# Rows of streamed operands at one byte of a 128-byte line

## Chip, cores, metric

One core of one Trainium2 chip. The metric is the device time of one execution in microseconds; the median of several runs counts.

## What is computed

Two blocks of a transformer over x of 256 rows and 1024 channels, all in float32. The first block has two layers, each a SwiGLU feed-forward, a mixer (a pooling mixer in the first layer, native sparse attention in the second), cross attention to a memory of 256 rows, and a second feed-forward. The second block has one layer: three kinds of attention side by side, gated and merged, and a feed-forward with squared ReLU. Cut to what carries the time:

```python
def swiglu_ffn(h, w_in, w_out):
    g, u = jnp.split(h @ w_in, 2, axis=-1)
    return (jax.nn.silu(g) * u) @ w_out

for i in range(2):
    x = x + 0.5 * swiglu_ffn(rms_norm(x, ffn1_norm[i]), ffn1_w_in[i], ffn1_w_out[i])
    x = x + mixer(rms_norm(x, mix_norm[i]))
    x = x + memory_cross_attention(rms_norm(x, xattn_norm[i]), rms_norm(mem, mem_norm[i]), ...)
    x = x + 0.5 * swiglu_ffn(rms_norm(x, ffn2_norm[i]), ffn2_w_in[i], ffn2_w_out[i])
# second block: u @ w_in feeds three attentions and their gates, then
h = jnp.square(jax.nn.relu(u2 @ w_ff1))
x = x + gate2 * (h @ w_ff2)
```

## The kernel before

Activations stand transposed: channels on the 128 partitions, the 256 rows of x on the free axis. Weights come from HBM in slabs of 1 MB (`raw`, L114), eight tiles of 128 channels by 256 columns, over SyncE's queue. ScalarE rounds a half slab to float32r (`wh`, L98), VectorE subtracts that from the slab (`wl`, L104). A float32 product is then three matmuls, `mm3` (L154, its matmuls are L157 to L159): `wh` with the activations' high part, `wh` with their low part, `wl` with the high part. In each the weight tile of 128 x 128 is loaded first, and the activations, 128 partitions x 256 columns, are streamed; the load for the next matmul runs beside the matmul that streams. A few products have it the other way round, with the activations loaded and the weights streamed (`row_tiles`, L603).

The activations that most slabs take are `xsh` and `xsl`, eight tiles (k = 0 to 7) of 256 columns. They lie in the pool `ac`, in a tile with two more columns in each row (`wide`, L283), which only the second block uses: there a product takes 258 columns. So row k begins 258 x 4 = 1032 bytes behind row k - 1. `pair` (L277) hands out such a tile for the tag `xs` and a packed one, 1024 bytes from row to row, for all others: `xs2h`/`xs2l` of the second block, `msh`/`msl` of the memory, `qT`. Temporaries of a phase come from `tmp` (L61): `hh`/`hl`, the inner activations of a feed-forward, `h2h`/`h2l` of the last one, `pTh`/`pTl`, `vh`/`vl` and `oh`/`ol` of the cross attention, and in the last feed-forward `xsh`/`xsl` too, packed.

Pools lie one behind the other in SBUF: `cst` (constants; its last tile is `fgg`, L1126), `wp` (slabs and split weights), `ac`, the pools of a block, and the pool of a phase. Inside a pool each tile takes its size, rounded up to 32 bytes a partition; a tag with two buffers has them side by side. Adding these up gives the byte at which rows begin. It is shown in a 128-byte line, and as the distance from the loaded weight tile to the streamed row, modulo 512 bytes (weight tiles are 512 bytes wide, so one number holds for all of a slab):

| operand, streamed | byte in the line | distance to the weights |
|---|---|---|
| `wh`, `wl` (loaded) | 96 | |
| `xsh` row k, `xsl` row k, wide | 96 + 8k, 32 + 8k | 8k, 64 + 8k |
| `hh`, `hl`, and packed `xsh`, `xsl` of the last feed-forward | 32 | 320 |
| `oh`, `ol` of the cross attention | 32 | 64 |
| `ms` of the merge | 32 | 192 |
| `xs2`, `ms` of the memory, `nsa_oh` | 96 | 128 |
| `h2h`, `h2l`, `nsa_ol` | 96 | 384 |
| `pTh`, `pTl` with `vh`, `vl` loaded, each with the next load | 32 (weights 32) | 0 |

In a feed-forward (`_swiglu`, L381) slab j goes: 96 matmuls with `xs` (for each of the eight k two column tiles of the gate and the up half, three matmuls each), then 48 with `hh`/`hl` of slab j - 2 (`output`, L410). The order of the work on each engine is the order of the program text; nothing in it depends on where tiles lie, except that a tile which takes another's place waits for that one's last reader.

Of the kernel before, what the change touches and what calls it, by code (L numbers as in the profile page):

```python
# [15 lines left out]
P = 128  # L16
# [4 lines left out]
F2 = 4096  # L21
EPS = 1e-6
# [4 lines left out]
class Slab:  # L27
    """A split weight slab in parts of n of its rows of tiles: (hi, lo) of columns c of row k."""
# [11 lines left out]
class Net:  # L40
    """Activations live transposed (channels on partitions, rows on the free axis). A float32
    product is three float32r passes over exactly split operands: hi*hi + lo*hi + hi*lo."""
# [18 lines left out]
    def tmp(self, shape, dtype=F32, tag="t", bufs=None, pool=None):  # L61
        kw = {} if bufs is None else {"bufs": bufs}
        return (pool or self.tp).tile(shape, dtype, tag=tag, name=self.name(tag), **kw)
# [5 lines left out]
    def phase(self, name, banks=0):  # L69
        """Temporaries of one phase, and PSUM banks beside the four of self.pm."""  # L70
# [9 lines left out]
    @contextmanager  # L80
    def banks(self, n):
        """n PSUM banks beside the four of self.pm, for one phase."""
        with self.tc.tile_pool(name=self.name("pa"), bufs=n, space=bass.MemoryType.PSUM) as pool:
            yield pool

    def fill(self, n=1):
        """Trace n steps of the work that waits for a gap on the tensor engine."""
# [26 lines left out]
    def raw(self, src, shape):  # L114
        """A weight slab as it is."""
# [10 lines left out]
    def slab(self, src, shape, perm=(None, None)):  # L126
        """A weight slab [128, ...], at most 8 KB a partition, from DRAM and split."""
        return self.split_slabs([self.raw(src, shape)], perm)[0]

    def split_slabs(self, raws, perm=(None, None), turn=1):  # L130
        """Slabs of one shape that are used side by side; turn = -1: from the last rows on."""
# [5 lines left out]
    def halves(self, raw, src=None, dst=None):  # L137
        """(hi, lo) of a part of a slab; src and dst give the views that are split one by one."""
# [15 lines left out]
    def mm3(self, out, w, x, start, stop, skip=True):  # L154
        """out += w.T @ x for split w and x."""
# [6 lines left out]
    def setup(self):  # L162
        """Constants, and x: transposed, and split for the first layer's feed-forward."""
# [10 lines left out]
        # the activation tables come while x does  # L174
# [4 lines left out]
        with self.phase("setup", 4) as px:  # L179
            # tiles k and k + 2 share a bank  # L180
# [11 lines left out]
            for h in range(2):  # L192
                # x's tiles and the slabs' parts in the order of their use
# [12 lines left out]
    def first_slabs(self):  # L206
        """The first slabs of the first feed-forward, in halves as they are needed."""
# [7 lines left out]
    def setup2(self):  # L215
# [12 lines left out]
        # rows that see no compressed block, and the blocks a row doesn't see  # L228
# [11 lines left out]
    def load_rows(self, src, dst):  # L240
        """[1, 256, 1024] of DRAM into dst [128, 8, 256], transposed."""
# [17 lines left out]
    def vector_columns(self, nm, vr):  # L259
        """Vectors of DRAM as columns: entry [p, i] of a vector's block is its value i*128+p."""  # L260
# [8 lines left out]
    def transpose2(self, dst, srcs):  # L269
        """dst [128, len(srcs)*128] from [128, 128] blocks."""  # L270
# [12 lines left out]
    def wide(self, tag, dtype):  # L283
        """Eight tiles of 256 columns and two more."""
        return self.ac.tile([P, KT, S + 2], dtype, tag=tag, name=self.name(tag))

# [1 line left out]
    def split(self, src, gain=None, tag="xs", pool=None, order=None):  # L288
        """(hi, lo) of src [128, n, 256] times a gain column per tile."""
# [8 lines left out]
    def rsqrt(self, y, v, eng):  # L298
        """y = 1/sqrt(v) on a few columns, from v/2 in v: a guess from the exponent, three Newton
        steps y*(v/2*y*y - 1.5), each of which turns the sign."""  # L300
# [3 lines left out]
        if eng is self.nc.vector:  # L304
            # column by column, which don't wait for one another
# [13 lines left out]
    def squares(self, src, tags=None):  # L319
        """Squares of src [128, n, 256], added over n: [128, 256]; tags: of the phase's [128, 2, 256]  # L320
        temporaries that serve."""
# [21 lines left out]
    def row_rstd(self, sq, n, ps, eng=None):  # L343
        """1/rms by row [128, 2] from the squares added over channel tiles, of n channels."""
# [10 lines left out]
    def on_rows(self, out, rn):  # L355
        """out [128, 256], in PSUM: the rows' values rn [128, 2] on all partitions."""
# [4 lines left out]
    def all_rstd(self, rn, ps):  # L361
        """1/rms on all partitions [128, 256]."""
# [5 lines left out]
    def rstd(self, src, between=None):  # L368
        """1/rms of every row: on all partitions [128, 256], and by row [128, 2]."""
# [103 lines left out]
    def sums(self, ps, cols, each, then=None):  # L473
        """For a loop over the channel tiles m of x: each(m), then x's squares summed over all
        channels, times columns, in ps [:, row half, column]; with None: the rest of them."""
# [31 lines left out]
    def _pool_mixer(self, gain, after):  # L507
# [25 lines left out]
        # the longest windows first  # L533
# [25 lines left out]
    def memory(self):  # L559
        """The memory, transposed and over its rows' rms."""  # L560
# [12 lines left out]
    def mem_kv(self, l):  # L573
        """Yields after every weight slab; ends with kT [128, 8, 256] and v [128, 2, 1024]."""
# [21 lines left out]
    def col_tiles(self, ps, ws, xs, n=KT, c=0):  # L596
        """ps [128, 2*256]: column tiles c, c+1 of a slab, transposed."""
# [5 lines left out]
    def row_tiles(self, ps, ws, xs):  # L603
        """ps [128, 2*256]: the product with a [1024, 256] slab, rows on partitions."""
# [9 lines left out]
    def _xattn(self, pa, l):  # L614
        nc, a = self.nc, self.a
        # x's tiles in the order in which they come
# [3 lines left out]
        # queries without their norm, which the softmax's scale by row takes  # L620
# [108 lines left out]
    # ---- native sparse attention  # L729
# [7 lines left out]
    def _nsa(self, ac, xs, sq, after):  # L737
        """Heads go in pairs (group 2a, r), (group 2a+1, r): one on the lower, one on the upper
        half of the partitions, so that queries and keys share them."""
# [1004 lines left out]
```

## Time and profile before

| what | value |
|---|---|
| median of 3 runs | 1582.18 us (1581.75 to 1584.72) |
| the profiled execution, from its first to its last instruction | 1590.3 us |
| TensorE busy | 1558.1 us, 12979 matmuls |
| VectorE, ScalarE, GpSimd busy | 1120.5, 831.0, 115.4 us |
| granted TensorE clock, mean | 0.994 |
| HBM read | 289.42 MB |

The page gives the busy time of each engine, the span in 40 slices, the chain of work that ended last, and the costliest groups of instructions. A group's mean duration is that of one instruction from its start to its modelled end; matmuls overlap, so the interval between two starts is shorter than that, and it is read from the timeline.

### The profile page before, as it was taken

The page shows a single profiled execution, that of the slowest core. Times are in us where ns is not written, and L with a number is a line of the kernel's source. Part 1 is how long each engine was busy: PE and PEld are TensorE (multiplying, and loading weights), DVE is VectorE, ACT ScalarE, POOL GpSimd, SP SyncE. Part 2 cuts the span into 40 slices and gives each one's busy share as a digit, 9 for nine tenths or more (in the row PEclk, how much of TensorE's full clock was granted, in tenths as well). Part 3 has the DMA queues.
Part 4 walks back from the last instruction along what each step waited for, and adds up shares of the span by engine and source line. Part 5 has one row for each costly group of instructions (what it writes and reads, how often), then busy time and mean ns, then how long its engine had stood idle before and what let it go on. Part 6 is the DMA issues. An engine that isn't in the chain of part 4 may idle for free.

```text
span 1590.3 us, 31387 instructions
## 1 busy us (share of the span) xinstructions
PE 1558.1 (98%) x12979; PEld 1523.9 (96%) x12979; DVE 1120.5 (70%) x2034; ACT 831.0 (52%) x1401; POOL 115.4 (7%) x195
## 2 busy tenths in 40 slices
PE   8999999999999999999999998999999999999998
PEld 8999999999999999999986997999999999999998
DVE  6676589688787688885677666887587755885553
ACT  6544457554445444453467554444453786464443
POOL 3010022030001100011000213000000000000000
PEclk9999999999999999999999999999999999999999
DMA  8645655457776677766741335686644644545540
GB/s 267 232 167 177 206 172 168 132 182 248 248 246 214 214 241 248 254 212 195 212 107 54 132 108 164 212 266 226 202 140 127 189 138 155 184 159 188 186 160 27
DMA packets 232364, 292.52 MB, mean 184 GB/s; under 512 B 7805, under 2 KB 210460, under 8 KB 232220
## 3 DMA queue, kind: packets, MB, share of 16 engines
q1 hardware_dynamic: 231756, 289.84, 56.2%
q8 instruction: 102, 1.67, 0.4%
q10 hardware_dynamic: 464, 0.66, 0.1%
q14 instruction: 42, 0.34, 0.1%
HBM read 289.42 MB, written 1.07 MB: 183 GB/s over the span
## 4 chain that ended last, share of the span: by engine, by line
PE 89%; DVE 4%; ACT 3%; POOL 2%; issue 1%; DMA 1%; DVEq 0%; ACTq 0%; POOLq 0%
PE ps L157 28%; PE ps L158 27%; PE ps L159 27%; DVE wl L104 1%; ACT wh L98 1%; PE tr L1392 1%; PE ps L874 1%; PE o L935 1%; PE ps L483 1%; ACT pn L957 0%; DVE isc L1477 0%; DVE iwk L1485 0%; DMA dl<-in_diff_lambda_dram 0%; POOL s L339 0%; PE ps L358 0%
## 5 line engine op out<-in xcount | busy, mean ns | idle before, releaser
L98 ACT CAST wh<-raw 128x1024 fp32r<-128x1024 f32 (+1 forms) x500 | 506.7, 1028 | 569.3 <-PE ps L158 459.2
L104 DVE TENSOR_TENSOR wl<-raw,wh 128x1024 fp32r<-128x1024 f32 (+1 forms) x500 | 605.9, 1225 | 256.9 <-ACT wh L98 256.1
L157 PE MATMUL ps<-xsh,wh 128*128 128x256 f32 (+1 forms) x1928 | 546.5, 283 | 0.9 <-ACT wh L98 0.9
L159 PE MATMUL ps<-xsh,wl 128*128 128x256 f32 (+1 forms) x1928 | 543.6, 282 | 0.7 <-DVE wl L104 0.7
L158 PE MATMUL ps<-xsl,wh 128*128 128x256 f32 (+1 forms) x1928 | 543.1, 282 | 0.0
L157 PEld LDWEIGHTS ps<-xsh,wh 128*128 128x128 f32 x1928 | 364.9, 189 | 2.1 <-ACT wh L98 1.2
L159 PEld LDWEIGHTS ps<-xsh,wl 128*128 128x128 f32 x1928 | 364.8, 189 | 1.1 <-DVE wl L104 1.1
L158 PEld LDWEIGHTS ps<-xsl,wh 128*128 128x128 f32 x1928 | 364.7, 189 | 0.0
L159 PE MATMUL ps<-hh,wl 128*128 128x256 f32 x704 | 197.4, 280 | 0.0
L157 PE MATMUL ps<-hh,wh 128*128 128x256 f32 x704 | 197.3, 280 | 0.0
L158 PE MATMUL ps<-hl,wh 128*128 128x256 f32 x704 | 196.8, 280 | 0.0
L158 PEld LDWEIGHTS ps<-hl,wh 128*128 128x128 f32 x704 | 132.8, 189 | 0.0
L159 PEld LDWEIGHTS ps<-hh,wl 128*128 128x128 f32 x704 | 132.2, 188 | 0.0
L157 PEld LDWEIGHTS ps<-hh,wh 128*128 128x128 f32 x704 | 131.9, 187 | 0.2
L157 PE MATMUL ps<-xs2h,wh 128*128 128x256 f32 x320 | 92.4, 289 | 0.0
L158 PE MATMUL ps<-xs2l,wh 128*128 128x256 f32 x320 | 90.9, 284 | 0.0
L159 PE MATMUL ps<-xs2h,wl 128*128 128x256 f32 x320 | 90.8, 284 | 0.0
L1027 DVE SCALAR_TENSOR_TENSOR moda<-raw,cs,moda 128x256 f32<-128x256 f32 x168 | 81.2, 483 | 4.5
L399 DVE TENSOR_TENSOR gu<-ps,rb 128x512 f32<-128x512 f32 x88 | 58.7, 687 | 29.0 <-PE ps L159 26.1
L158 PE MATMUL ps<-h2l,wh 128*128 128x256 f32 x256 | 72.1, 282 | 0.1
L157 PE MATMUL ps<-h2h,wh 128*128 128x256 f32 x256 | 72.2, 284 | 0.0
L159 PE MATMUL ps<-h2h,wl 128*128 128x256 f32 x256 | 72.1, 282 | 0.0
(420 smaller groups left out, 2629.0 us busy)
## 6 DMA issues: line engine op xcount, KB each, us to landing
raw<-in_ffn_w_in_dram SPq DMA_DIRECT2D x86, 1024.0 KB, 6.4
raw<-in_ffn_w_out_dram SPq DMA_DIRECT2D x44, 1024.0 KB, 7.2
raw<-in_w_ff_dram SPq DMA_DIRECT2D x32, 1024.0 KB, 5.3
raw<-in_ada_w_dram SPq DMA_DIRECT2D x24, 1024.0 KB, 6.9
raw<-in_w_in_dram SPq DMA_DIRECT2D x24, 1024.0 KB, 5.2
raw<-in_xattn_w_kv_dram SPq DMA_DIRECT2D x16, 1024.0 KB, 7.4
raw<-in_nsa_w_in_dram SPq DMA_DIRECT2D x10, 1024.0 KB, 5.6
raw<-in_xattn_w_q_dram SPq DMA_DIRECT2D x8, 1024.0 KB, 5.1
```

Source lines behind the costliest of these rows:

```text
L98: return self.nc.scalar.copy(out, x)
L104: return self.nc.vector.tensor_tensor(out, x, h, ALU.subtract)
L157: mm(out, w[0], x[0], start=start, stop=False, skip_group_check=skip)
L158: mm(out, w[0], x[1], start=False, stop=False, skip_group_check=skip)
L159: mm(out, w[1], x[0], start=False, stop=stop, skip_group_check=skip)
L399: nc.vector.tensor_tensor(gu, ps.rearrange("p (h s) -> p h s", h=2), rb2, ALU.mult)
L483: nc.tensor.matmul(ps[:, r * n:(r + 1) * n], sq[:, r * P:(r + 1) * P], cols[:, k], start=(k == r == 0), stop=(k == KT - 1), skip_group_che ...
L874: nc.tensor.matmul(ps[:, m * 64:m * 64 + 60], w1s[j // 8][:, j % 8, m * P:(m + 1) * P], blk[:, j], start=(j == 0), stop=(j == 15))
L935: nc.tensor.matmul(o[half * 64:half * 64 + 64, (r % 2) * S + kt * P:(r % 2 + 1) * S], vS[:, i, kt, g * 64:(g + 1) * 64], pT[:, :S] if kt = ...
L1027: nc.vector.scalar_tensor_tensor(acc, raw[:, k], cs[:, k:k + 1], acc, ALU.mult, ALU.add)
L1392: nc.tensor.transpose(ps[:, j * P:(j + 1) * P], p[:, j * P:(j + 1) * P], self.ident)
```

## The change

`wide` gives a row 288 columns instead of 258 and hands out the first 258 of them, so row k begins 1152 bytes behind row k - 1. `tmp` rounds every temporary up to 32 columns (128 bytes) and hands out a view of the shape that was asked for. The constant `fgg` of 8 columns gets room for 24, and `iw`, 2 x 8 columns, gets rows of 16. No instruction is added or taken away. The rest of the diff takes comments and docstrings out, and isn't shown.

```diff
+LINE = 32
...
     def tmp(self, shape, dtype=F32, tag="t", bufs=None, pool=None):
         kw = {} if bufs is None else {"bufs": bufs}
-        return (pool or self.tp).tile(shape, dtype, tag=tag, name=self.name(tag), **kw)
+        n = math.prod(shape[1:])
+        t = (pool or self.tp).tile([shape[0], -(-n // LINE) * LINE], dtype, tag=tag, name=self.name(tag), **kw)[:, :n]
+        if len(shape) == 2:
+            return t
+        names = "abcd"[:len(shape) - 1]
+        return t.rearrange(f"p ({' '.join(names)}) -> p {' '.join(names)}", **dict(zip(names, shape[1:])))
...
-        return self.ac.tile([P, KT, S + 2], dtype, tag=tag, name=self.name(tag))
+        return self.ac.tile([P, KT, S + LINE], dtype, tag=tag, name=self.name(tag))[:, :, :S + 2]
...
-        self.fgg = self.cst.tile([P, KT], F32, name="fgg")
+        self.fgg = self.cst.tile([P, 24], F32, name="fgg")[:, :KT]
...
-        iw = a2.tile([P, 2, 8], F32, name="iw")
+        iw = a2.tile([P, 2, LINE // 2], F32, name="iw")[:, :, :8]
```

The same adding up for the changed sizes: the pool behind `cst` begins 64 bytes later, so `wh` and `wl` begin at byte 32 of a line, and so does every streamed row. The distances become 0, 128, 256, 384, 0, ... for rows 0, 1, 2, 3, 4, ... of the wide `xsh` and `xsl`; 256 for `hh`, `hl`, `oh`, `ol` and the packed `xsh`, `xsl`; 0 for `xs2`, the memory's `ms`, `nsa_oh` and `h2`; 128 for the merge's `ms`; 384 for `nsa_ol`.

## Rows read from the trace of the kernel before

**Rows 1.** The page: busy time, granted clock, chain by engine and by line.
```profile
PE 1558.1 (98%) x12979; PEld 1523.9 (96%) x12979; DVE 1120.5 (70%) x2034; ACT 831.0 (52%) x1401; POOL 115.4 (7%) x195
...
PEclk9999999999999999999999999999999999999999
...
PE 89%; DVE 4%; ACT 3%; POOL 2%; issue 1%; DMA 1%; DVEq 0%; ACTq 0%; POOLq 0%
PE ps L157 28%; PE ps L158 27%; PE ps L159 27%; DVE wl L104 1%; ACT wh L98 1%; PE tr L1392 1%; PE ps L874 1%; PE o L935 1%; PE ps L483 1%; ACT pn L957 0%; DVE isc L1477 0%; DVE iwk L1485 0%; DMA dl<-in_diff_lambda_dram 0%; POOL s L339 0%; PE ps L358 0%
```
**Rows 2.** Who waited for whom: us in total, times, longest us.
```profile
ACT wh L98 <- PE ps L158: 459.2, 210, 5.2
```
**Rows 3.** Timeline, TensorE, one feed-forward slab: start us, us, operands.
```profile
439.74 0.28 PE L157 MATMUL ps<-hh,wh 128*128 128x256 f32 x1
...
445.40 0.28 PE L157 MATMUL ps<-xsh,wh 128*128 128x256 f32 x1
...
446.81 0.28 PE L157 MATMUL ps<-xsh,wh 128*128 128x256 f32 x1
...
448.24 0.28 PE L157 MATMUL ps<-xsh,wh 128*128 128x256 f32 x1
...
449.66 0.28 PE L157 MATMUL ps<-xsh,wh 128*128 128x256 f32 x1
...
451.10 0.28 PE L157 MATMUL ps<-xsh,wh 128*128 128x256 f32 x1
...
452.51 0.28 PE L157 MATMUL ps<-xsh,wh 128*128 128x256 f32 x1
...
453.95 0.28 PE L157 MATMUL ps<-xsh,wh 128*128 128x256 f32 x1
...
455.38 0.28 PE L157 MATMUL ps<-xsh,wh 128*128 128x256 f32 x1
...
456.82 0.28 PE L157 MATMUL ps<-hh,wh 128*128 128x256 f32 x1
```
**Rows 4.** Timeline, TensorE, last feed-forward: 48 matmuls between each two rows.
```profile
1520.40 0.28 PE L157 MATMUL ps<-xsh,wh 128*128 128x256 f32 x1
...
1526.06 0.28 PE L157 MATMUL ps<-h2h,wh 128*128 128x256 f32 x1
...
1531.75 0.28 PE L157 MATMUL ps<-xsh,wh 128*128 128x256 f32 x1
```
**Rows 5.** Timeline, TensorE, cross attention: 12 matmuls between the two rows.
```profile
306.50 0.28 PE L157 MATMUL ps<-pTh,vh 128*128 128x256 f32 x1
...
307.90 0.28 PE L157 MATMUL ps<-oh,wh 128*128 128x256 f32 x1
```
**Rows 6.** Matmuls by line and form: count, busy us, mean ns, idle before.
```profile
L157 PE MATMUL ps<-xsh,wh 128*128 128x256 f32 x1888 | 534.9, 283 | 0.9 <-ACT wh L98 0.9
...
L157 PE MATMUL ps<-hh,wh 128*128 128x256 f32 x704 | 197.3, 280 | 0.0
...
L157 PE MATMUL ps<-xs2h,wh 128*128 128x256 f32 x320 | 92.4, 289 | 0.0
...
L157 PE MATMUL ps<-h2h,wh 128*128 128x256 f32 x256 | 72.2, 284 | 0.0
...
L157 PE MATMUL ps<-msh,wh 128*128 128x256 f32 x192 | 54.6, 285 | 0.0
...
L157 PE MATMUL ps<-wh,msh 128*128 128x256 f32 x128 | 36.6, 286 | 0.0
```
**Rows 7.** ScalarE by line and form: split writes at staggered and at aligned rows.
```profile
L99 ACT ACTIVATE xsh<-xT,v 128x256 fp32r<-128x256 f32 x48 | 21.7, 502 | 9.5 <-DVE xT L469 4.2 <-DVE xT L471 3.8 <-DVE xT L531 1.3
...
L99 ACT ACTIVATE msh<-memT,v 128x256 fp32r<-128x256 f32 x16 | 7.0, 501 | 2.7 <-DVE memT L570 1.4 <-PE ps L158 1.3
```
**Rows 8.** Timeline, TensorE, sparse attention's values: 47 intervals between the two rows.
```profile
772.12 0.28 PE L157 MATMUL ps<-wh,xsh 128*128 128x256 f32 x1
...
777.65 0.28 PE L159 MATMUL ps<-wh,xsl 128*128 128x256 f32 x1
```

## The prediction

> **What bounds the kernel now.** I read the page's table of busy time first, then the chain that ended last, then the waits, and only then single instructions. TensorE is busy 98% of the 1590.3 us span, the clock granted to it is full (the 2.4 GHz level) in every slice, and 89% of the chain is TensorE, nearly all of it the three lines of `mm3` [rows 1]. ScalarE, which splits the weights, waits 459.2 us for TensorE to give their buffers back [rows 2]. So the time is the sum of the intervals from one matmul's start to the next's, and an edit that changes that interval changes the time one for one. The mean durations in the groups (280 to 289 ns) are no guide, since matmuls overlap; the interval is read from start times in the timeline.
>
> The intervals differ, with the same shape, the same clock and no gap. In one feed-forward slab 48 matmuls that stream `hh`/`hl` take 445.40 - 439.74 = 5.66 us, 117.9 ns each; the 96 behind them, which stream `xsh`/`xsl`, take 456.82 - 445.40 = 11.42 us, 119.0 ns each [rows 3]. Row by row (12 matmuls each) the rows k = 0, 2, 4, 6 take 1.41, 1.42, 1.41, 1.43 us, the rows 1, 3, 5, 7 take 1.43, 1.44, 1.44, 1.44: 118.1 ns against 119.8. Even rows begin at a multiple of 16 bytes, odd ones 8 bytes off it (the table of bytes stands ahead). In the last feed-forward, where `xsh` has its own packed tile, 48 matmuls take 1526.06 - 1520.40 = 5.66 us, 117.9 ns, and the 48 with `h2h`/`h2l` 1531.75 - 1526.06 = 5.69 us, 118.5 ns [rows 4]. Both stream packed, 32-byte-aligned rows against the same weight buffers; they differ in the byte of the 128-byte line (32 and 96, the weights being at 96).
>
> **The change part by part.** No instruction, transfer or semaphore is added or removed; every instruction keeps its shape. What changes is where tiles lie.
>
> Part 1, stride 288 for `wide`, the columns of `fgg` and the rounding in `tmp`, seen from TensorE. Behind `fgg` everything moves 64 bytes on, so the weights go from byte 96 to byte 32 and all streamed rows come to byte 32 too. The trace has little in which both streams begin at one byte. I order it by the distance from the weights that are loaded meanwhile to the streamed row, modulo 512 bytes: `hh` and the packed `xsh` have 320, `h2` and the other tiles at byte 96 have 128 or 384, and one group has 0: `pTh`/`pTl` with `vh`/`vl` in the cross attention, 12 matmuls in 307.90 - 306.50 = 1.40 us, 116.7 ns [rows 5]. That is a short group, so I take 117.4, between it and the 117.9. After the change, by adding up the tiles: rows k = 0 and 4 of `xs`, `xs2`, `h2` and the memory's `ms` have distance 0; rows 2 and 6, `hh` and the packed `xsh` have 256; odd rows of `xs` and the merge's `ms` have 128 or 384. No row shows 256; I take it as now for aligned rows, 117.9, with 117.4 and 118.5 as ends.
>
> Counts [rows 6]: `xs` with the wide stride 1888 less the last feed-forward's 14 slabs x 16 = 1664 triples, 4992 matmuls; `hh` 704 and the packed `xsh` 224 triples, 2784 matmuls; `xs2` 320, `h2` 256, memory `ms` 128 as streamed and 128 as stationary operand (rest of 192: the merge's 64), 832 triples, 2496 matmuls.
> - `xs`: (2 x 117.4 + 2 x 117.9 + 4 x 118.5)/8 = 118.1, from 119.0: 0.9 x 4992 = 4.4 us off.
> - tiles at byte 96: from 118.5 to 117.4: 1.1 x 2496 = 2.8 us off.
> - `hh` and packed `xsh`: nothing; ends -0.5 and +0.6 ns, -1.4 and +1.7 us.
> - the merge, 192 matmuls, to 118.5: 0.1 us on.
> Sum: 7.1 us off.
>
> Part 2, the engines that write and read these rows. `xsh` is now written at rows 8 bytes apart in the line, `msh` at aligned ones, by the same operation: 502 and 501 ns [rows 7]. So alignment costs ScalarE nothing, and I cost the rest at nothing. It is hidden under TensorE anyway: ScalarE and VectorE are busy 52% and 70%. Were that cover gone, as where splits stand on the chain (3% and 4%), the 1 ns between the two rows over 48 writes would be 0.05 us. The DMAs' target moves by 64 bytes with the size of its rows unchanged; DMA is 1% of the chain.
>
> Part 3, the layout. Small temporaries grow from 32 to 128 bytes and the wide pair by 1920 bytes, so a later phase's tiles lie over other tiles of the phase before, and may wait for another last reader. The trace can't show that; the waits of TensorE on a split at a slab's start add up to 0.9 us in the largest group [rows 6], so I allow 1 us either way and take 0.
>
> The profiled execution lasts 1590.3 us as a span, of which the median of 1582.18 us is 99.5%; the difference is carried over whole: 1582.2 - 7.1 = 1575.1 us, taken as 1575.
>
> **Rivals.**
> 1. Only the streamed row's own byte counts. Then all aligned rows at byte 32 take 117.9: `xs` 1.1 x 4992 = 5.5, tiles at 96 0.6 x 2496 = 1.5, together 7.0 us off, 1575.2. For it: rows 4, where the weights are common. Against it: with `wh`/`wl` streamed from byte 96 over `xs` as the stationary operand 47 intervals take 777.65 - 772.12 = 5.53 us, 117.7 ns [rows 8], where `h2` at that byte takes 118.5. The time is the forecast's. The Trainium skill ("TensorE: Matmul & The Clock Gate", Part 2, step-by-step) says that weights are loaded through a read port of their own and take nothing from the running matmul; by that, this rival would hold, and rows 8 speak against it.
> 2. Only a start off a multiple of 16 bytes costs. Then odd rows come to the even ones' 118.1, all else stays: 1.7 x 2496 = 4.2 us off, 1578.0. For it: the even and odd rows [rows 3]; against it: `xsh` and `h2`, both on such multiples, 117.9 and 118.5 [rows 4]. The Trainium skill ("SBUF — State Buffer", Specifications (TRN2)) gives SBUF lines of 16 bytes and a penalty for each crossing; this is that rule's outcome, and rows 4 show more than it holds.
> 3. One byte for both streams is itself what costs: `h2` and the weights are both at 96, and 118.5 is the price whatever the distance. Then `xs` gains 0.5 x 4992 = 2.5, `hh` and the packed `xsh` lose 0.6 x 2784 = 1.7: 0.8 us off, 1581.4. For it: rows 4; against it: rows 5, both streams at byte 32 or 0 modulo 128 from each other, and fast.
> 4. Slower: with every stream at one byte, the moving row and the weight load ask for the same part of SBUF at the same time in each of some 10,300 matmuls, and it costs what the dearest rows show, 119.8. Place: `mm3`; price: 0.8 x 4992 + 1.9 x 2784 + 1.3 x 2496 = 12.5 us, 1594.7. It decides once the mean over these three groups, now (119.0 x 4992 + 117.9 x 2784 + 118.5 x 2496)/10272 = 118.6, rises above that; over 118.9 it is measurable. For it: the trace shows distance 256 nowhere and 0 only in short groups.
> 5. The change does nothing that counts (rows move, intervals stay, waits from the layout eat the rest): 1582.
>
> **How the numbers follow.** The forecast has 0.48 and rival 1 0.10, both at 1575; rival 2 0.10 at 1578; rival 3 0.14; rival 4 0.12; rival 5 0.06. The lowest bound is 117.4 for all three groups: 8.0 + 1.4 + 2.8 = 12.2 us off, 1570, less 1 for the layout and 1 for smaller groups that I left out (258 columns, `nsa_oh`): 1568. The upper end takes rival 3 and 5 in, and rival 4 where it costs a third: 1586. About 0.2% (3.2 us) is what a measurement can tell from no change: faster, below 1579.0, is the forecast with rivals 1 and 2, less what the bounds leave doubtful, 0.66; same 0.21; slower 0.13.
>
> **What would show it.** In the timeline after, a feed-forward slab's 96 `xs` matmuls take 11.34 us (11.42 before), with odd rows at 1.42 us and rows 0 and 4 at 1.41; `h2`'s 48 take 5.64 and `xs2`'s likewise; `hh`'s 48 stay at 5.66. ACT `xsh` stays near 502 ns and TensorE at 98%. `h2` at 5.69 with `hh` at 5.69 means rival 3; `hh` at 5.75, rival 4; only odd rows faster, rival 2. The prediction fails if distance 256, which no row shows, is dear: it carries `hh`, the packed `xsh` and two rows of `xs`.

## The result, and the profile after

| kernel | median | runs | lowest to highest |
|---|---|---|---|
| before | 1583.41 us | 9 | 1581.75 to 1594.90 |
| after | 1594.15 us | 9 | 1591.86 to 1602.64 |

The ratio is 1.0061 [1.0043, 1.0079]: the change makes the kernel 0.6% slower, some 9.7 us (6.8 to 12.5), where 7 us off were predicted. 1594.15 lies above the range of 1568 to 1586.

The two profiled executions differ by 2.1 us only (1590.3 and 1592.4). That is no measure of the change, for at one place TensorE waited long in the one of before and hardly in the one of after. The row of before, then that of after (timeline, TensorE; start us, us, operands, and in brackets the idle time ahead of it and what ended it):

```profile
988.25 1.23 PE L358 MATMUL ps<-ident,rn 128*128 128x128 f32 x4 [7.49 <-POOL rn L317]
```
```profile
986.17 0.71 PE L364 MATMUL ps<-ident,rn 128*128 128x128 f32 x4 [1.03 <-POOL rn L323]
```

7.49 us of waiting for GpSimd in one, 1.03 in the other. It is a matter of the execution: the same kernel has it in one and not in another (below, under the runs with the gap of 192 bytes). With these 6.5 us set right the spans differ by 8.6 us, near what the ratio says. The starts of the same matmul in both traces say it more closely: just ahead of the wait the changed kernel is 4.4 us behind, 50 matmuls after it 2.6 us ahead, at the end 2.1 us behind; without the wait and what it leaves behind it is 9.0 us longer.

The page of the kernel after, in the lines that answer to [rows 1], and the wait that answers to [rows 2]. In the changed kernel `mm3`'s matmuls are L163 to L165 and the writers of the splits L104 and L110, 6 lines further down.

```profile
PE 1566.8 (98%) x12979; PEld 1532.8 (96%) x12979; DVE 1122.3 (70%) x2034; ACT 831.5 (52%) x1401; POOL 111.3 (7%) x195
...
PEclk9999999999999999999999999999999999999999
...
PE 91%; DVE 3%; ACT 3%; POOL 1%; DMA 1%; issue 1%; DVEq 0%; ACTq 0%; POOLq 0%
```
```profile
ACT wh L104 <- PE ps L164: 400.7, 192, 4.8
```

Nothing in these lines names a cause. The instructions are the same, the granted clock is at 90% or more in every slice, VectorE and ScalarE are as busy as before. TensorE is busy 8.7 us more (1566.8 against 1558.1) with the same 12979 matmuls. The loss is seen in the starts of single matmuls. One feed-forward slab, where `hh` takes 48 matmuls and `xsh` 96 [rows 3]; 48 each of `h2` and the packed `xsh` in the last feed-forward [rows 4]; and the 12 of `pTh` with `vh` in the cross attention [rows 5] (timeline, TensorE):

```profile
441.98 0.28 PE L163 MATMUL ps<-hh,wh 128*128 128x256 f32 x1
...
447.72 0.28 PE L163 MATMUL ps<-xsh,wh 128*128 128x256 f32 x1
...
459.15 0.28 PE L163 MATMUL ps<-hh,wh 128*128 128x256 f32 x1
```
```profile
1515.96 0.28 PE L163 MATMUL ps<-h2h,wh 128*128 128x256 f32 x1
...
1521.72 0.28 PE L163 MATMUL ps<-xsh,wh 128*128 128x256 f32 x1
...
1527.48 0.29 PE L163 MATMUL ps<-h2h,wh 128*128 128x256 f32 x1
```
```profile
308.01 0.28 PE L163 MATMUL ps<-pTh,vh 128*128 128x256 f32 x1
...
309.45 0.28 PE L163 MATMUL ps<-oh,wh 128*128 128x256 f32 x1
```

`hh` takes 5.74 us (119.6 ns each, 117.9 before), `xsh` 11.43 us (119.1; 119.0 before). In the last feed-forward both operands take 5.76 us, 120.0 ns, where it was 118.5 and 117.9. `pTh` takes 1.44 us, 120.0 ns, against 116.7.

Over all stretches of each group, worked out from the differences of the starts (ns; the distances, modulo 512 bytes, are those of the tables ahead):

| streamed | matmuls | before: distance, ns | after: distance, ns | us |
|---|---|---|---|---|
| `hh`, packed `xsh` | 2784 | 320, 117.8 | 256, 119.75 and 120.0 | +5.5 |
| `xs2`, `h2`, memory's `ms` (also as loaded operand) | 2496 | 128 and 384, 118.7 | 0, 119.9 | +3.1 |
| `oh` of the cross attention | 384 | 64, 117.8 | 256, 119.9 | +0.8 |
| merge's `ms` | 192 | 192, 117.5 | 128, 118.8 | +0.3 |
| wide `xs` | 4992 | 8k and 64 + 8k, 118.96 | 0, 128, 256, 384, 118.9 | -0.3 |

The sum is 9.4 us. So the loss is where the forecast had nothing (`hh` and the packed `xsh`) or a gain (`h2` and its like), and the gain of `xs`, the larger part of the forecast, did not come.

### The profile page after: what moved, and what is told of

Same layout as the page of the kernel before. It is cut to its first block, busy times and chain, and to the rows that moved or that the text cites. A ratio compares the mean times of both kernels' runs of the same rounds, so it can differ in the third digit from the quotient of the medians.

```text
span 1592.4 us, 31389 instructions
## 1 busy us (share of the span) xinstructions
PE 1566.8 (98%) x12979; PEld 1532.8 (96%) x12979; DVE 1122.3 (70%) x2034; ACT 831.5 (52%) x1401; POOL 111.3 (7%) x195
## 4 chain that ended last, share of the span: by engine, by line
PE 91%; DVE 3%; ACT 3%; POOL 1%; DMA 1%; issue 1%; DVEq 0%; ACTq 0%; POOLq 0%
PE ps L163 28%; PE ps L164 28%; PE ps L165 28%; ACT wh L104 1%; PE tr L1398 1%; PE ps L880 1%; DVE wl L110 1%; PE o L941 1%; DMA raw<-in_ada_w_dram 1%; PE ps L489 1%; ACT pn L963 0%; POOL s L345 0%; PE ps L929 0%; POOL vh L345 0%; PE pi L163 0%
## 5 line engine op out<-in xcount | busy, mean ns | idle before, releaser
L104 ACT CAST wh<-raw 128x1024 fp32r<-128x1024 f32 (+1 forms) x500 | 505.9, 1027 | 541.8 <-PE ps L164 400.7
L110 DVE TENSOR_TENSOR wl<-raw,wh 128x1024 fp32r<-128x1024 f32 (+1 forms) x500 | 604.8, 1222 | 255.9 <-ACT wh L104 255.0
L163 PE MATMUL ps<-xsh,wh 128*128 128x256 f32 (+1 forms) x1928 | 546.9, 284 | 1.6 <-ACT wh L104 0.8
L165 PE MATMUL ps<-xsh,wl 128*128 128x256 f32 (+1 forms) x1928 | 544.4, 282 | 0.0
L163 PEld LDWEIGHTS ps<-xsh,wh 128*128 128x128 f32 x1928 | 365.4, 190 | 3.1 <-ACT wh L104 1.2
L165 PEld LDWEIGHTS ps<-xsh,wl 128*128 128x128 f32 x1928 | 364.5, 189 | 0.3 <-DVE wl L110 0.3
L163 PE MATMUL ps<-hh,wh 128*128 128x256 f32 x704 | 199.5, 283 | 0.0
L165 PE MATMUL ps<-hh,wl 128*128 128x256 f32 x704 | 199.1, 283 | 0.0
L163 PEld LDWEIGHTS ps<-hh,wh 128*128 128x128 f32 x704 | 134.7, 191 | 0.1
L165 PEld LDWEIGHTS ps<-hh,wl 128*128 128x128 f32 x704 | 134.8, 191 | 0.0
L163 PE MATMUL ps<-xs2h,wh 128*128 128x256 f32 x320 | 92.7, 290 | 0.0
L165 PE MATMUL ps<-xs2h,wl 128*128 128x256 f32 x320 | 91.2, 285 | 0.0
L165 PE MATMUL ps<-h2h,wl 128*128 128x256 f32 x256 | 72.4, 284 | 0.0
L163 PE MATMUL ps<-h2h,wh 128*128 128x256 f32 x256 | 72.4, 285 | 0.0
```

What stands on the lines that cost most here:

```text
L104: return self.nc.scalar.copy(out, x)
L110: return self.nc.vector.tensor_tensor(out, x, h, ALU.subtract)
L163: mm(out, w[0], x[0], start=start, stop=False, skip_group_check=skip)
L165: mm(out, w[1], x[0], start=False, stop=stop, skip_group_check=skip)
```

## The experiments

The theory after the result: what sets the interval is the distance between the loaded weight tile and the streamed row, modulo some power of two, and 0 and 256 are the dear ones. The rivals: the byte in the 128-byte line, the row stride, or the new layout as a whole.

**The byte alone.** Before, with `fgg` enlarged as in the change. Weights and streamed rows all move 64 bytes on; bytes change, distances don't.

```diff
-        self.fgg = self.cst.tile([P, KT], F32, name="fgg")
+        self.fgg = self.cst.tile([P, 24], F32, name="fgg")[:, :KT]
```

> The kernel before, with fgg at 24 columns and nothing else: everything behind the constants moves 64 bytes, so weights go from byte 96 of a 128-byte line to 32 and every streamed row moves with them; all distances between the two stay. If the distance sets the interval: no change (within 0.1%), hh and the packed xsh stay at 117.9 ns from start to start, h2 and xs2 at 118.5. If the byte itself sets it: hh, now at 96, goes to 118.5 and h2, now at 32, to 117.9, or, if weights at 32 are what costs, all of them to about 120.

1584.3 us, ratio 1.0009 [0.9995, 1.0022]. The last feed-forward (timeline, TensorE):

```profile
1504.46 0.28 PE L157 MATMUL ps<-h2h,wh 128*128 128x256 f32 x1
...
1510.14 0.28 PE L157 MATMUL ps<-xsh,wh 128*128 128x256 f32 x1
...
1515.80 0.28 PE L157 MATMUL ps<-h2h,wh 128*128 128x256 f32 x1
```

`h2`, now at byte 32, takes 5.68 us (118.3), `xsh`, now at byte 96, 5.66 us (117.9): they have swapped the bytes and kept the intervals of [rows 4]. So the byte alone does nothing.

**The stride alone.** Before, with rows of 288 columns in `wide` and nothing else.

```diff
-        return self.ac.tile([P, KT, S + 2], dtype, tag=tag, name=self.name(tag))
+        return self.ac.tile([P, KT, S + 32], dtype, tag=tag, name=self.name(tag))[:, :, :S + 2]
```

> The kernel before, with the row stride of 288 columns alone. Bytes of all tiles behind the wide pair stay (h2 and xs2 at 96, hh at 32, weights at 96), but the pair's 1920 more bytes move their distances by 384 modulo 512: xs2 and the memory's ms 128 to 0, h2 384 to 256, hh and the packed xsh 320 to 192. If the distance modulo 256 sets the interval: xs2, ms and h2 go from 118.5 to 120.0 (1.5 ns x 2496 = 3.7 us), hh stays at 117.9, wide xs stays at 119.0, in all 3 to 5 us slower (1587). If only the distance modulo 128 or the byte counts: h2 and xs2 stay at 118.5 and the time is that of the kernel before.

1574.33 us, ratio 0.9946 [0.9929, 0.9962]: faster where 3 to 5 us slower were expected: a miss. Last feed-forward (timeline, TensorE):

```profile
1517.11 0.28 PE L157 MATMUL ps<-h2h,wh 128*128 128x256 f32 x1
...
1522.86 0.29 PE L157 MATMUL ps<-xsh,wh 128*128 128x256 f32 x1
...
1528.31 0.28 PE L157 MATMUL ps<-h2h,wh 128*128 128x256 f32 x1
```

`h2` (distance 256) takes 5.75 us, 119.8 ns, as expected. The packed `xsh`, which with `hh` has come to distance 192, takes 5.45 us: 113.5 ns, lower than any interval of before. Over all stretches `hh` has 113.6. So the sum is -4.2 x 2784 = -11.7 us, +1.1 x 2496 = +2.7 and -1.4 x 384 = -0.5 for `oh`, -9.5 against the 8.6 measured. No row of before has this price; the distance was there only in the merge, where it took 117.5. One part of the change gains 9 us, then, and the rest (`fgg`, `iw` and the rounding in `tmp`), which brings `hh` and the packed `xsh` from 192 to 256 and `oh` from 448 to 256, costs 18 us by the ratios and 20 by the medians.

**The changed kernel, moved by 64 bytes.** A pool of 64 bytes between the weights and everything streamed: weights stay at byte 32, all rows at byte 96.

```diff
         self.wp = pool("wp", 3)
+        pool("gap", 1).tile([P, 16], F32, name="gap")
         self.ac = pool("ac", 1)
```

> The changed kernel with 64 unused bytes between the weights' pool and the activations: weights stay at byte 32, every streamed row goes to byte 96, all distances are 64 more (64, 192, 320 or 448). If the distance is what costs in the changed kernel: every group at 117.8 to 117.9 ns, so 1.1 x 4992 + 2.0 x 2784 + 2.1 x 2496 = 16 us off the changed kernel, 1578 or a little less, and about 7 us under the kernel before (0.45%). If aligned rows, padded temporaries or the layout of the phases are what costs: it stays near 1593.

1567.61 us, ratio 0.9891 [0.9877, 0.9905], some 10 us less than the 1578 expected. In its profiled execution (8.6 ms) TensorE started a matmul 640 ns after the other throughout; its page has no row of the granted clock, so what slowed it stays open, and no interval is read from it. The same kernel once more:

> The same kernel as e3_gap64, for a trace at the full clock (the profiled execution of e3_gap64 ran on a slowed TensorE throughout). Time again near 1567. If distances set the intervals, the timeline shows which groups are under the 117.9 ns that was forecast for distances 64, 192, 320, 448: 1567 instead of 1575 needs some of them near 113.

1565.12 us, ratio 0.9875 [0.986, 0.989]. A slab, and the last feed-forward (timeline, TensorE):

```profile
438.90 0.28 PE L164 MATMUL ps<-xsh,wh 128*128 128x256 f32 x1
...
450.02 0.28 PE L164 MATMUL ps<-hh,wh 128*128 128x256 f32 x1
...
1498.60 0.28 PE L164 MATMUL ps<-h2h,wh 128*128 128x256 f32 x1
...
1504.25 0.28 PE L164 MATMUL ps<-xsh,wh 128*128 128x256 f32 x1
```

`h2` at 64 takes 117.7 ns (5.65 us) where 0 took 120.0, and the 96 of `xs`, now at 64, 192, 320, 448 in turn, 11.12 us: 115.8. Over all slabs without a gap, the rows at 64 and 320 take 117.8 and those at 192 and 448 take 114.8, which is why the time came out below the expectation. The odd multiples of 64 are the cheap ones here, and 64 unused bytes are worth 27 to 29 us.

**A series for each distance.** Behind the last product of before, series of 48 matmuls with `dwh`, `dwl` loaded and `dxh`, `dxl` streamed in the order of `mm3`; from series to series only the distance changes. Their results are not used.

```diff
+            for n, (dh, dl) in enumerate(points):
+                xs = [x[0][:, dh // 4:dh // 4 + S], x[1][:, dl // 4:dl // 4 + S]]
+                for i in range(16):
+                    c = slice(i % 8 * P, i % 8 * P + P)
+                    for j, (wt, xt) in enumerate(((w[0], xs[0]), (w[0], xs[1]), (w[1], xs[0]))):
+                        nc.tensor.matmul(o, wt[:, c], xt, start=(i == j == 0), stop=(i == 15 and j == 2), ...)
```

> The kernel before and behind it 26 series of 48 matmuls of mm3's kind, at chosen distances from loaded weights to streamed row (work added, nothing left out): 0, 8, 16, 24, 32, 48, 64, 80, 96, 112, 128, 160, 192, 224, 256, 320, 384, 448 for high and low part alike, then pairs (high, low) (0,128), (64,192), (0,64), (32,160), (128,0), (64,128), (96,224), (0,192). If the distance modulo 256 sets the interval: 0 and 256 at 120.0 ns, 128 and 384 at 118.6, 64, 192, 320, 448 at 117.8, the multiples of 32 between near 118, and 8 and 24 dearer than 16. Modulo 128: 0, 128, 256, 384 alike. If distance is nothing and the neighbourhood (other engines, waits) makes the difference: all alike. About 26 x 5.7 = 148 us longer.

The first matmul of some of the series (timeline, TensorE; 48 matmuls to the next series, at the distances 112, 192, and 256, 320, 384, 448):

```profile
1639.30 0.28 PE L1658 MATMUL dps<-dxh,dwh 128*128 128x256 f32 x1
...
1644.73 0.28 PE L1658 MATMUL dps<-dxh,dwh 128*128 128x256 f32 x1
...
1656.12 0.28 PE L1658 MATMUL dps<-dxh,dwh 128*128 128x256 f32 x1
...
1661.77 0.28 PE L1658 MATMUL dps<-dxh,dwh 128*128 128x256 f32 x1
...
1667.45 0.28 PE L1658 MATMUL dps<-dxh,dwh 128*128 128x256 f32 x1
...
1673.20 0.28 PE L1658 MATMUL dps<-dxh,dwh 128*128 128x256 f32 x1
...
1678.86 0.28 PE L1658 MATMUL dps<-dxh,dwh 128*128 128x256 f32 x1
...
1684.56 0.28 PE L1658 MATMUL dps<-dxh,dwh 128*128 128x256 f32 x1
...
1690.03 0.28 PE L1658 MATMUL dps<-dxh,dwh 128*128 128x256 f32 x1
```

5.43 us at 112, 5.65 at 192; then 5.75 at 256, 5.66 at 320, 5.70 at 384, 5.47 at 448. The mean interval in the last three quarters of each series, where it is settled: 8, 24, 80, 96 and 256 have 120.0; 128 and 384 118.7; 64, 192 and 320 117.8; 448 and 112 113.3; 16 and 32 116.7. The very first series, at 0, began at the granted clock's lower level (0.50, 1.2 GHz) with 213 ns from start to start; its last 20 matmuls, at 2.4 GHz, have 120.0. In the kernel before and after the groups at 0, 256, 128, 384, 64 and 320 have these numbers within 0.3 ns. Shapes and operations are the same in all of them.

The series with the high part at one distance and the low part at another say that a mixture is no mean: (0, 128), high part first, took 117.8 and (0, 64) 117.8, both less than the 120.0 and 118.7 of 0 and 128 alone, but (128, 0) took 119.9.

The distance 192 had 117.8 here and 113.6 in the run with the stride alone. So series were run again, each distance behind series at 0, at 64 and at 112:

> The kernel before and behind it 45 pairs of series of 48 matmuls: each distance (0, 16, 32, 48, 64, 96, 112, 128, 160, 176, 192, 224, 240, 320, 448) three times, behind a series at 0, at 64 and at 112. If a distance has one interval, its three series agree with each other (0 at 120.0, 64 and 320 at 117.8, 112 at 113.3, 192 and 448 alike). If the state in which a series begins decides too, 192 comes out at 117.8 behind one and near 113.5 behind another, as hh in e2_wide_only (113.6 at 192) and in the first curve (117.7 at 192, 113.3 at 448).

The first matmuls of the series at 0 and then 128, and at 192 (timeline, TensorE):

```profile
1823.35 0.28 PE L1660 MATMUL dps<-dxh,dwh 128*128 128x256 f32 x1
...
1829.11 0.28 PE L1660 MATMUL dps<-dxh,dwh 128*128 128x256 f32 x1
...
1834.81 0.28 PE L1660 MATMUL dps<-dxh,dwh 128*128 128x256 f32 x1
...
1930.94 0.29 PE L1660 MATMUL dps<-dxh,dwh 128*128 128x256 f32 x1
...
1936.40 0.28 PE L1660 MATMUL dps<-dxh,dwh 128*128 128x256 f32 x1
```

5.76 us at 0, 5.70 at 128, as before; but 5.46 at 192, and settled 113.3 behind all three, where the first series had 117.8 (that one stood behind a series at 160). Series at 0 settled at 120.0, whatever stood ahead, but for the first of the run, which again began at 213 ns. At 16 a series behind 64 took 116.7, behind 0 or 112 118.6; at 32 one behind 0 took 117.8, behind 64 or 112 116.7. So some distances have two steady values, and as far as single series show it what ran just before chooses; 0 has one, and no distance took longer.

**Is it the distance, or the stride?** Before, with a gap of 384 bytes: the row stride stays 258 columns, `hh` and the packed `xsh` come to 192, `h2` to 256, the memory's `ms` and `xs2` to 0.

```diff
         self.wp = pool("wp", 3)
+        pool("gap", 1).tile([P, 96], F32, name="gap")
         self.ac = pool("ac", 1)
```

> The kernel before with 384 unused bytes between the weights' pool and the activations: stride of 258, no rounding, every byte in the 128-byte line as before; distances as in e2_wide_only for all but the wide pair (hh and packed xsh 192, h2 256, xs2 and the memory's ms 0). If the distance modulo 512 makes hh fast and h2 slow in e2_wide_only: hh and packed xsh near 113.6 (4.2 ns x 2784 = 11.7 us off), h2, xs2, ms near 119.8 (1.3 x 2496 = 3.2 us on), about 1575. If the aligned stride of xs does it: hh stays at 117.9, h2 and xs2 go to 119.8, about 1587.

1578.61 us, ratio 0.9974 [0.9953, 0.9995]. (timeline, TensorE)

```profile
437.32 0.28 PE L158 MATMUL ps<-hh,wh 128*128 128x256 f32 x1
...
442.76 0.28 PE L158 MATMUL ps<-xsh,wh 128*128 128x256 f32 x1
...
454.26 0.28 PE L158 MATMUL ps<-hh,wh 128*128 128x256 f32 x1
...
1499.05 0.28 PE L158 MATMUL ps<-h2h,wh 128*128 128x256 f32 x1
...
1504.79 0.29 PE L158 MATMUL ps<-xsh,wh 128*128 128x256 f32 x1
```

`hh` takes 5.44 us (113.3), `h2` 5.74 (119.6): what the distance gives, with the old stride. The time lies between the two that were expected, because the wide `xs`, whose rows keep their steps of 8 bytes and only start elsewhere, went from 119.0 to 119.7 (11.50 us for 96 in this slab), 4 us that the expectation had not counted.

**Another gap, and a control.** The changed kernel with gaps of 192 and of 256 bytes (`[P, 48]` and `[P, 64]` in the line above). 192 brings `h2` and its like to 192, `hh` to 448. 256 only exchanges the distances 0 and 256.

> The changed kernel with 192 unused bytes in the gap instead of 64: distances hh and packed xsh 448, xs2, ms and h2 192, xs 192, 320, 448, 64, ... by row. If only the distance modulo 128 counts, it is e3_gap64 again, 1567. If modulo 256, hh (448 as 192) takes what xs2 and h2 (64) take there and the other way round. In any case under the kernel before, since no distance is a multiple of 128.

> The changed kernel with the gap of 192 bytes once more, beside the row stride of 320 columns on the same chip: 1555 to 1566 us, as before, with hh at 448 and h2 at 192 bytes between 113.3 and 117.8 ns.

> The changed kernel with a gap of 256 bytes, where 64 and 192 were tried: every streamed row moves 256 bytes on, so hh and the packed xsh come from distance 256 to 0, h2, xs2 and ms from 0 to 256. If the distance modulo 256 sets the interval, nothing changes against the changed kernel: 119.8 to 120.0 ns in all these groups, 1592 to 1597 us. If a gap helps because it moves the tiles behind the weights at all, whatever its size, the time comes to the 1555 to 1568 us of the gaps of 64 and 192 bytes.

With 192: 1560.45 us, ratio 0.9857 [0.9828, 0.9887], and on another chip 1565.47, 0.9876 [0.9862, 0.9891]. With 256: 1593.1 us, ratio 1.0058 [1.004, 1.0076], the time of the changed kernel. So neither a gap as such nor the moved layout behind it costs or gains time; what does is where the distances stand modulo 256. The last feed-forward with 256 (timeline, TensorE):

```profile
1491.55 0.28 PE L164 MATMUL ps<-h2h,wh 128*128 128x256 f32 x1
...
1497.31 0.28 PE L164 MATMUL ps<-xsh,wh 128*128 128x256 f32 x1
...
1503.07 0.28 PE L164 MATMUL ps<-h2h,wh 128*128 128x256 f32 x1
```

5.76 us and 5.76 us, as after. And with 192 (first run), `hh` in a slab and the packed `xsh` of the last feed-forward, both at distance 448:

```profile
398.01 0.28 PE L164 MATMUL ps<-hh,wh 128*128 128x256 f32 x1
...
403.66 0.28 PE L164 MATMUL ps<-xsh,wh 128*128 128x256 f32 x1
...
1496.14 0.28 PE L164 MATMUL ps<-xsh,wh 128*128 128x256 f32 x1
...
1501.58 0.28 PE L164 MATMUL ps<-h2h,wh 128*128 128x256 f32 x1
```

5.65 us (117.7) in the one, 5.44 (113.3) in the other: the two values again, and a whole block of 48 has one or the other. The profiled executions of the two runs, 1553.0 and 1566.4 us, differ by more than half through the wait for GpSimd that was shown above, 0.97 us in the first, 8.59 in the second, with nearly the same intervals on the whole (115.7 and 115.8 ns). So that wait comes and goes from one execution of a kernel to another; the profiled executions of the shift of all bytes, the stride alone and the gap of 384 bytes have it too (7.6, 8.2 and 8.4 us). What makes GpSimd late wasn't looked into.

**All rows at cheap distances.** The gap of 192 with a stride of 320 columns: 1280 bytes, so that the rows of `xs` alternate between 192 and 448. To make room, small temporaries of the cross attention (`rs`, and in lines not shown `rsq`, `rn` and `rv`) get one buffer in place of two.

```diff
-        return self.ac.tile([P, KT, S + LINE], dtype, tag=tag, name=self.name(tag))[:, :, :S + 2]
+        return self.ac.tile([P, KT, S + 64], dtype, tag=tag, name=self.name(tag))[:, :, :S + 2]
...
-        rs = self.tmp([P, 2, 2], tag="rs")
+        rs = self.tmp([P, 2, 2], tag="rs", bufs=1)
```

> The changed kernel with the gap of 192 bytes, and a row stride of 320 columns (1280 bytes) for the wide tiles in place of 288, so that the rows of xs alternate between the distances 192 and 448 and never come to 64 or 320; three small temporaries of the cross attention have one buffer in place of two, to make room. If a distance has an interval of its own, the rows at 64 and 320 (2496 of 4992 matmuls, 117.8 ns in the run with the gap alone) take what 192 and 448 took there, 115.0: 2.8 x 2496 = 7.0 us off, 1553 with the 1560 of that run. If 192 and 448 have two values (113.3 and 117.8 in the series) and a row at 64 or 320 leaves the pair in the slower one, all rows go to 113.3: 4.5 x 2496 + 1.7 x 2496 = 15.5 us off, 1545. If only the streamed row's own byte in its line of 128 bytes counts, nothing changes: 1560, since all rows are at the same byte in both.

1555.61 us (1545.47 to 1560.83), ratio 0.9814 [0.9785, 0.9843], on a chip where the gap alone has 1565.47: 9.9 us off by the medians, and 7.4 between the two profiled executions (1559.0 and 1566.4), which both have the wait for GpSimd. Of that, 2.6 x 2496 = 6.5 us are the rows that were at 64 and 320 (117.8 to 115.2). 192 and 448 went on taking either 113.3 or 117.8 by whole blocks, so the hope for 113.3 everywhere falls. A slab, and a row some slabs later (timeline, TensorE, and from the waits of 395 to 470 us; there: who waited for whom, us in total, times, longest us):

```profile
378.01 0.28 PE L164 MATMUL ps<-hh,wh 128*128 128x256 f32 x1
...
383.45 0.28 PE L164 MATMUL ps<-xsh,wh 128*128 128x256 f32 x1
...
394.33 0.28 PE L164 MATMUL ps<-hh,wh 128*128 128x256 f32 x1
...
407.32 0.39 PE L166 MATMUL ps<-xsh,wl 128*128 128x256 f32 x1 [1.18 <-DVE wl L111]
```
```profile
ACT wh L105 <- DMA raw<-in_ffn_w_in_dram: 20.1, 8, 3.3
...
PE ps L166 <- DVE wl L111: 3.6, 4, 1.2
```

A slab's `hh` and `xs` take 5.44 and 10.88 us, 113.3 ns for all 144. Some slabs later TensorE waits for the split of the weights, and the split for the slab's DMA. In these 75 us TensorE's matmuls lose 3.6 us to that. In the changed kernel itself ScalarE waits as long for the slabs of the matching stretch (23.1 us, 9 times, from 400 to 476 us) and TensorE not at all: at 113 ns a matmul it reaches the weights before they are split.

**Which tile of weights?** The prediction took the distance to the tile that is loaded meanwhile, not to the one in use. Within a slab, with both parts of a row at one distance, the two are the same modulo 512, since weight tiles are 512 bytes wide. In this run weights and row walk on together, by 64 or 16 bytes a matmul, so that the two distances differ and stay constant.

```diff
+                for i in range(48):
+                    a = i * step // 4
+                    b = d // 4 + min(i + 1, 47) * step // 4
+                    nc.tensor.matmul(o, w[:, a:a + P], x[:, b:b + S], start=(i == 0), stop=(i == 47), ...)
```

> The kernel before, and behind its last product 56 series of 48 matmuls (256 columns, one row each). In 28 of them the weights and the streamed row walk on together by 64 or 16 bytes a matmul, so that the row has one constant distance to the weights that are loaded meanwhile (the next matmul's) and another to the weights in use. If the load that runs beside the matmul decides, as the prediction took it: step 64 with 0 to the loaded and 64 to the used weights takes 120.0 ns; 448 to the loaded, 0 to the used 113.3; 64 to the loaded, 128 to the used 117.8; 384 to the loaded, 448 to the used 118.7. If the weights in use decide: 117.8, 120.0, 118.7 and 113.3. If neither does and it is the row's place alone, the walking series all come out alike. Series without a step, as in the runs before: 0 120.0, 64 117.8, 112 and 448 113.3.

Settled intervals, worked out from the starts, with (distance to the tile being loaded, to the tile in use): (0, 64) 117.6, (64, 128) 117.5, (128, 192) 119.8, (192, 256) 118.6, (384, 448) 119.8, (448, 0) 118.6. The expectation by the loaded tile was 120.0, 117.8, 118.7 and 113.3 for the first, second, fifth and sixth; that by the tile in use 117.8, 118.7, 113.3 and 120.0. The first fits the tile in use and the second the loaded one; (384, 448) and (448, 0) fit neither. The series with a step of 16 are as mixed: (0, 16) 118.7, (112, 128) 118.9, (96, 112) 117.1, (496, 0) 117.2. That pairs 256 bytes apart agree, (128, 192) with (384, 448) and (192, 256) with (448, 0), shows the period of 256 once more. Without a step 0 had 120.0 (but for the first series), 112 and 448 113.3, and 64 had 117.8 fifteen times and 113.3 once, behind a series that walked. How the loaded tile, the used tile and the row together make the interval stays open, and so does what picks one of two values.

## Why the prediction was wrong

What bounds the kernel was right: from before to after no engine but TensorE moved the time, and an interval that changes by 1 ns moves it by 1 ns a matmul (9.4 us by the groups, 9.0 by the two traces, 9.7 by the ratio). Only the clock was read too simply: it was not full throughout, for in the trace before it was granted at 0.50 around the wait for GpSimd, 984.8 to 991.7 us. That is worth some 0.5 us there (4.4 + 2.6 - 6.5) and moves nothing in the sum. To order the rows by the distance and not by the byte was right too; the shift of all bytes shows it. What failed are the prices put on two distances.

1. **Distance 256, `hh` and the packed `xsh`.** "No row shows 256; I take it as now for aligned rows, 117.9, with 117.4 and 118.5 as ends." It took 119.75 to 120.0. This one step is +5.5 us, more than half of the loss. Its ends came from aligned groups alone; the intervals that the trace did show for this shape went up to 119.8 (the odd rows in [rows 3]), and for an unknown price that end belonged into the range. The prediction's last sentence named the step as the one on which it fails.
2. **Distance 0, the tiles at byte 96.** 117.4 was taken from `pTh` with `vh` [rows 5]; it took 119.9, so +3.1 us in place of -2.8. The row was no case of distance 0 alone. By adding up the tiles, its high and low parts lie 128 bytes apart modulo 512 and come by turns, so the distance is always 0 to the tile being loaded, but 0, -128 and 128 in turn to the one in use. After the change the parts lie at one byte, both distances are 0, and the same 12 matmuls take 120.0 ns (the rows of 308.01 us above); that a mixture of 0 and 128 can take less than either is what the series (0, 128) shows, with 117.8. That the distance to the loaded tile alone counts was an assumption that nothing in the trace had tested, and the walking series don't bear it out.
3. **The wide `xs`.** 0.9 x 4992 = 4.4 us were to come off, from rows at 0 and 256 taking 117.4 and 117.9 and the others 118.5. Over the slabs whose 96 matmuls run without a gap (30 before, 31 after; worked out from the starts) the odd rows went from 119.9 to 119.0, so some of their gain came, and the even rows, now at 0 and 256, from 117.9 to 119.1 and took it back: the price of these two distances once more. Row 0, behind `hh` at 256, takes 120.0 in all its 12 matmuls; rows 2, 4 and 6, each behind a row at 128 or 384, take 118.2 in the first five and 120.0 from the ninth on. At 128 and 384 a pattern of five intervals repeats, 118.7 on average. So in this layout a row is too short to pay 120.0 in full, and the 119.0 before was a mean over rows at sixteen distances.
4. **What was left out.** `oh` of the cross attention went from 64 to 256, +0.8 us; the merge was put at +0.1 and took +0.3.
5. **ScalarE and the layout.** Both were right at nothing. ScalarE's writes of the splits, which answer to [rows 7], by line and form:

```profile
L105 ACT ACTIVATE xsh<-xT,v 128x256 fp32r<-128x256 f32 x48 | 21.7, 501 | 9.0 <-DVE xT L475 4.3 <-DVE xT L477 3.4 <-DVE xT L537 1.2
...
L105 ACT ACTIVATE msh<-memT,v 128x256 fp32r<-128x256 f32 x16 | 6.9, 500 | 2.9 <-PE ps L164 1.5 <-DVE memT L576 1.4
```

501 and 500 ns, 502 and 501 before. The control with 256 bytes shows that another layout at the same distances costs nothing.

Of the rivals the fourth, at 0.12, came nearest, and the sign named for it, `hh` at 5.75 us, came (5.74). Its price of 119.8 fits every group at 0 or 256 but the wide `xs` (119.75 to 120.0), and its 1594.7 stands beside 1594.15; but in part by luck, since it had 4.0 us for the wide `xs`, which on the whole paid nothing, started from a median 1.2 us lower, and left out `oh` and the merge. Its mechanism, that both streams ask for the same part of SBUF at the same time, is not shown: series at 8, 24, 80 and 96 took 120.0 as well. Its rule that this "costs what the dearest rows show" was the better way to price a case without rows. The first rival falls by the shift of all bytes. The Trainium skill ("TensorE: Matmul & The Clock Gate", Part 2, step-by-step) states that loading the next tile's weights takes no SBUF read bandwidth from the running matmul. By that it should not matter where the weights lie; the runs differ, for the distance to them moves the interval from 113.3 to 120.0 ns. The second rival falls too: every row is now on a multiple of 16 bytes, and though the odd rows of `xs` gained about 1 ns, the even ones, which stood on such multiples before, lost 1.2. The third, 118.5 for one byte, falls as the price is that of the distance, 120.0 at 0 and 256 and 118.7 at 128 and 384. The fifth falls by the result, 0.4 to 0.8% slower.

The chances said 0.13 for slower. That was too little for a forecast in which one main price stood on a 12-matmul row and another on no row.

## What to carry to other kernels

Where TensorE streams and loads without a pause, add up the addresses and look at the distance between weight tiles and streamed rows modulo 256 bytes: everything at one byte (0) was among the worst choices here, and with 64 bytes of padding between the two pools the changed kernel is 1.1 to 1.2% faster than before instead of 0.6% slower. "Aligned" says nothing by itself; a short series of the kernel's own matmuls at each distance, put behind its last product, prices it in one run, if the first series is left out and each distance stands behind more than one other. And a row stands for a case only if everything that the theory leaves out is also the same in it; where no row does, the range has to reach to the dearest interval that the trace shows for that shape.

## What the runs showed of the hardware

Float32r matmuls of 128 x 128 by 256 columns, each with its own weight load, at the granted clock's upper level, 2.4 GHz, don't have one interval: settled means from 113.3 to 120.0 ns were measured. At multiples of 64 bytes the price repeats every 256: 120.0 at 0, 117.8 at 64, 118.7 at 128, at 192 either 113.3 or 117.8. 64 also had 113.3 once, and the groups at 320 in the cross attention of the changed kernel with the gap of 64 bytes 113.9. Distances that are not such multiples range as far: 120.0 at 8, 24, 80 and 96, 116.7 or 118.6 at 16, 116.7 or 117.8 at 32, 113.3 at 112. The state outlasts other work in between: in the runs with the gap of 192 bytes `hh` stays at 117.8 for a run of slabs in one feed-forward and at 113.3 in another.

Behind the wait for GpSimd the next four matmuls took 1.23 us in one execution and 0.71 where the wait was short (the two rows at the top). What followed the longer idle time ran at the granted clock's lower level, 1.2 GHz: the clock granted from 988.25 to 991.50 us was 0.50 before and 1.00 after. At that level, in the first series of the runs with series, matmuls at distance 0 started every 213 ns, where 2.4 GHz gave 120.0.
